# The down projection of a decoder layer by Strassen's scheme: 20 of 22 inner tiles in five chunks instead of 16 in four, on one core

## The chip, the core and the metric

The kernel runs on one core of a Trainium2 chip. The core has five engines with a queue each, which works strictly in its written order: TensorE (PE, matmuls, with its weight loads shown as PEld), VectorE (DVE), ScalarE (ACT), GpSimd (POOL) and SyncE (SP, which here only issues transfers). The metric is the device time of one execution in microseconds, the median of several runs.

## The reference

One layer of a decoder trunk for 1024 prompt tokens and 8 sample tokens (T = 1032 columns), in fp32. The part that the change is about, word for word:

```python
x = x + cross_attn(rmsnorm(x, g_attn), mk, mv, w_q, w_o)
h = rmsnorm(x, g_ffn)
x = x + (jax.nn.silu(h @ w_gate) * (h @ w_up)) @ w_down
...
y_prompt = rmsnorm(xp, g_final)
y_sample = rmsnorm(xs, g_final)
```

The model's width is 1024 (8 tiles of 128), the inner width of the feed-forward part is 2816 (22 tiles of 128). Ahead of these lines come an input projection, a causal mean pooling, a depthwise convolution of width 31 with a layer norm, the output projection, and the keys and values of 256 memory tokens.

## The kernel before, in words

**Layout.** The activations lie transposed: channels on the 128 partitions, tokens along the free dimension. Tokens come in two halves of 512 and 520. An fp32 matmul is made of three passes (`PASSES`, L133): each operand is split into a high part and a rest of type fp32r, and high x high, high x rest and rest x high are added up in PSUM. To *split* an operand costs ACT one instruction (the high part) and DVE one (the rest), both in `split` (L458, instructions at L466 and L477); `split_by_dma` (L483) lets ACT write the high part and its negative, and POOL issues a transfer that adds the original on top (L495).

**Stages in time.** Input projection, convolution, pooling, keys and values (0 to about 225 us), output projection and queries, attention (about 350 to 420), its output projection (to about 515), gate and up (to about 905), down (to about 1067), the last tiles and the final norm.

**Gate and up** work on one pair of inner tiles after the other by Strassen's seven products (`seven`, L1571; `others`, L1534). What comes out is stored by `to_hidden` (L1552): for the inner tiles below `FIRST_LAST` (L147) as the seven operand blocks `hb` that the next Strassen scheme needs, per chunk of four inner tiles; for the tiles from `FIRST_LAST` on as plain tiles `hd`. A block that is listed in `SPLIT_BLOCKS` (L58) is split there (`to_blocks`, L1504) and stored twice, high part and rest; a tile in `SPLIT_FIRST` (L59) likewise.

**Down** runs over `CHUNKS` chunks (L147) of four inner tiles, and in each over four output pairs: units u = 0 to 15, `down(u)` (L1669). A unit makes seven products `pr` (`product`, L1407, matmuls at L1429): three operands of the seven are 512 tokens wide, four are 520 wide (two matmuls of 260). A unit has 18 matmuls of 512 columns and 48 of 260. Every product is added by DVE from PSUM onto the running sums `x2` and `pp` (`plus_sums`, L1445), in the first chunk in part copied by ACT (`copy_sums`, L1449). Weights are loaded, summed (`dt`, L1631, POOL or DVE) and split (`dW`, `dV`) by `dn_load` and `dn_prep` (L1615, L1619); the blocks by `down_blocks` (L1642), which loads both parts of a block that was split ahead, and else loads it once and splits it (`hs` -> `hb`).

**The last tiles.** The inner tiles 16 to 21 go the plain way: `last_down` (L1783) multiplies them in three token spans of 512, 260 and 260 columns, for each of the 8 output tiles 18 matmuls `fd` (L1800). DVE adds the result to `x2` (L1809), ACT squares it (L512) and scales it by the final norm's gain (L1818), POOL or DVE add the squares (L513). The running sums are brought together once for each output pair by `second_half` (L1706, three DVE additions of 520 each, L1453). After each span `final_factors` (L1821) sums over channels on PE, takes the root on ACT, and three DVE instructions make the factor (L1841, L1843, L1845); `final` (L1849) multiplies on DVE (L1854) and sends `out_yT`.

**What sets the order.** A planner at the kernel's start (`Program`, L171): tasks are entered in the order of the code (`ORDER`, L41, for the first half), get a priority from their number, an offset `NUDGE` (L72) and costs with `MARGINS` (L65), some of them a fixed engine (`CHOSEN`, L119). `order` (L216) issues one after the other the task that can start first, within `SLACK` (L62) the one with the lowest priority. Buffers are taken when the task is planned; products use two PSUM buffers of three banks (`mm`) and two of one bank (`ms`). What comes out is fixed: each engine's queue is in that order.

Of the kernel before, what the change touches and what calls it, by code (L numbers as in the profile page):

```python
# [48 lines left out]
BY_DMA = {"w_in": (0, 3, 4, 6, 7, 9, 10, 11), "w_k": (2, 3, 5), "w_o": (4, 5, 6), "w_out_a": (1,), "w_out_b": (3,), "w_q": (4, 5, 6), "w_v": (0, 7), "w_dn": (18, 19), "w_dn2": (1,)}
# [1 line left out]
LEAD = {"w_k": 4, "w_v": 7, "w_out_a": 16, "w_q": 42, "w_in": 22, "w_out_b": 11, "w_o": 14}
# [1935 lines left out]
```

## Time and profile before

| | before |
|---|---|
| median of 3 runs | 1146.24 us (1144.82 to 1146.77) |
| profiled execution | 1144.27 us |
| span of the profiled execution | 1142.5 us |
| matmuls `pr` of the down stage | 288 of 512 columns, 768 of 260 |
| matmuls `fd` of the last tiles | 144 of 512 columns, 288 of 260 |

How to read it: the span goes from the first to the last record of the profiled execution; its own time is 1.8 us longer. Busy times add up an engine's records, a busy PE is not PE at its peak, and an engine's idle time only counts where others wait for it. A group's row has the line, the engine, the operation, output<-inputs, the shapes and the count, then busy us, mean ns of one, and the idle time ahead of them with what ended it.

### The profile page before, as it was taken

The numbers are of one execution on the slowest core, as the hardware profiler recorded it, in microseconds if no ns is written. First come the engines' busy times: TensorE is split into PE (matmuls) and PEld (weight loads), VectorE is DVE, ScalarE is ACT, GpSimd is POOL, SyncE is SP. The second block draws the span as 40 slices with busy tenths as digits, with TensorE's granted clock in tenths as the row PEclk, the third lists the DMA queues.
The fourth block names the chain that finished last, engine by engine and source line by source line (L and its number), as shares of the span: only waits on it lengthen the run. The fifth ranks groups of instructions, "written<-read, shape, count | busy, mean of one in ns | idle before, by whom it ended". The sixth has DMA issues, their size and how long they took to land.

```text
span 1142.5 us, 19533 instructions
## 1 busy us (share of the span) xinstructions
PE 1120.8 (98%) x7736; PEld 1067.4 (93%) x7736; DVE 927.6 (81%) x1514; ACT 499.7 (44%) x706; POOL 287.8 (25%) x327
## 2 busy tenths in 40 slices
PE   9999999999999989999999999999999999999996
PEld 8999988999999979999999999999999999999996
DVE  7999999776257886888888888988888798879744
ACT  7766648353243452445233333333433443332444
POOL 2689772133712201433000000000000123332011
PEclk9999999999999999999999999999999999999999
DMA  8444587433485687322424352254433697657612
GB/s 307 94 93 110 127 233 237 163 114 149 165 249 176 207 325 244 123 82 75 140 84 149 128 190 105 100 176 159 156 124 112 237 374 286 242 169 235 186 59 91
DMA packets 66252, 193.54 MB, mean 169 GB/s; under 512 B 8368, under 2 KB 12144, under 8 KB 64880
## 3 DMA queue, kind: packets, MB, share of 16 engines
q1 hardware_dynamic: 62128, 178.81, 43.8%
q0 software_dynamic: 3600, 13.13, 6.6%
q8 instruction: 61, 1.00, 0.4%
q10 hardware_dynamic: 432, 0.36, 0.1%
q14 instruction: 31, 0.25, 0.1%
HBM read 147.84 MB, written 44.43 MB: 168 GB/s over the span
## 4 chain that ended last, share of the span: by engine, by line
PE 78%; DVE 15%; DMA 4%; issue 1%; ACT 1%; POOL 0%; DVEq 0%; SPq 0%; ACTq 0%; POOLq 0%
PE pr L1429 49%; PE po L582 7%; DVE cacc L783 6%; PE ps L582 5%; PE fd L1800 4%; PE oa L582 4%; PE ob L582 4%; DVE spcache_k L1223 1%; PE vps L1027 1%; DMA spcache_k<-in_cache_k 1%; PE kps L949 1%; PE pv L1184 1%; DVE spcache_v L1223 1%; DVE xss L513 1%; DVE x L1854 1%
## 5 line engine op out<-in xcount | busy, mean ns | idle before, releaser
L1429 PEld LDWEIGHTS pr<-ab,wTb 128*128 128x128 f32 x1056 | 123.4, 190 | 2.3 <-issue 0.5
L1429 PE MATMUL pr<-ab,wTa 128*128 128x260 f32 x1056 | 124.9, 275 | 0.0
L1429 PE MATMUL pr<-ab,wTb 128*128 128x260 f32 x1056 | 124.3, 275 | 0.0
L1429 PEld LDWEIGHTS pr<-ab,wTa 128*128 128x128 f32 x1056 | 123.1, 190 | 1.3
L1429 PE MATMUL pr<-ab,wG 128*128 128x512 f32 x528 | 121.1, 380 | 0.0
L1429 PEld LDWEIGHTS pr<-ab,wG 128*128 128x128 f32 x528 | 96.9, 189 | 12.5 <-issue 0.5
L582 PE MATMUL ps<-xop,w 128*128 128x344 f32 x720 | 105.5, 309 | 0.0
L582 PEld LDWEIGHTS ps<-xop,w 128*128 128x128 f32 x720 | 105.0, 189 | 0.0
L1445 DVE TENSOR_TENSOR su<-pr,su 128x520 f32<-128x520 f32 (+1 forms) x112 | 77.3, 692 | 25.9 <-PE pr L1429 25.4
L1429 PEld LDWEIGHTS pr<-hb,dV 128*128 128x128 f32 x768 | 92.3, 190 | 2.2
L1429 PE MATMUL pr<-hb,dV 128*128 128x260 f32 x768 | 92.7, 275 | 0.0
L582 PE MATMUL ps<-xq,w 128*128 128x344 f32 x576 | 87.0, 310 | 0.0
L582 PE MATMUL po<-oo,w 128*128 128x344 f32 x576 | 84.7, 309 | 0.0
L582 PEld LDWEIGHTS po<-oo,w 128*128 128x128 f32 x576 | 84.3, 189 | 0.2
L582 PEld LDWEIGHTS ps<-xq,w 128*128 128x128 f32 x576 | 84.2, 189 | 0.1
L783 DVE SCALAR_TENSOR_TENSOR cacc<-glu,vec,cacc 128x502 f32<-128x502 f32 (+14 forms) x116 | 77.5, 739 | 0.1
L1429 PE MATMUL pr<-hb,dW 128*128 128x512 f32 x288 | 69.2, 379 | 0.0
L1456 POOL MEMSET su<- 128x16 f32 x22 | 2.4, 112 | 255.7 <-PE pr L1429 200.1
L1800 PE MATMUL fd<-ho,w 128*128 128x260 f32 (+1 forms) x432 | 64.3, 311 | 0.0
L1800 PEld LDWEIGHTS fd<-ho,w 128*128 128x128 f32 x432 | 59.8, 190 | 4.4 <-issue 0.5
L1445 DVE TENSOR_TENSOR x<-pr,x 128x512 f32<-128x512 f32 (+1 forms) x76 | 52.3, 690 | 12.7 <-PE pr L1429 11.6
L766 POOL TENSOR_TENSOR y<-y,cp 128x511 f32<-128x511 f32 (+14 forms) x46 | 57.6, 1254 | 14.9 <-DVE y L766 7.2
(314 smaller groups left out, 2164.7 us busy)
## 6 DMA issues: line engine op xcount, KB each, us to landing
gr<-in_w_gu SPq DMA_DIRECT2D x44, 512.0 KB, 3.4
hb<-su SPq DMA_DIRECT2D x16, 520.0 KB, 3.8
hb<-hb SPq DMA_DIRECT2D x16, 520.0 KB, 6.7
dr<-in_w_dn SPq DMA_DIRECT2D x16, 512.0 KB, 4.0
hb<-bh SPq DMA_DIRECT2D x14, 520.0 KB, 3.3
hb<-hb SPq DMA_DIRECT2D x14, 512.0 KB, 7.4
spcache_k<-in_cache_k SPq DMA_DIRECT2D x12, 512.0 KB, 5.2
ho<-hd SPq DMA_DIRECT2D x10, 520.0 KB, 6.3
```

What stands on the lines that cost most here:

```text
L513: add({"Pool": pool_tt(n), "DVE": dve(n)}, lambda e: e.tensor_tensor(total(), total(), sq[:, i, :n], ALU.add), [(sq, i), tkey], [tkey], lo ...
L582: e.matmul(placed(ps[:, c, :CW]), w[:, wi, cols], turns(x[:, xi, c * CW : (c + 1) * CW]), start=first and p == 0, stop=last and p == 2)
L766: add({"Pool": pool_tt(HALF), "DVE": dve(HALF)}, lambda e: e.tensor_tensor(yb[:, i, HALF + n : SEQ], yb[:, i, HALF + n : SEQ], cp[:, q, : ...
L783: e.scalar_tensor_tensor(acc[h][:, n:], src[:, : HALF - n], w, acc[h][:, n:], ALU.mult, ALU.add)
L949: e.matmul(placed(ps[:, 0, i * NMEM : (i + 1) * NMEM]), w[:, wi, block_cols(k)], turns(memg[k // 4][:, xi, k % 4]), start=(k == 0 and p == ...
L1027: e.matmul(placed(ps[:, m]), memg[k // 4][:, xi, k % 4, m * P : (m + 1) * P], turns(w[:, wi, col : col + 512]), start=(k == 0 and p == 0), ...
L1184: e.matmul(placed(ps[:, c]), v[:, vi, m, col : col + P], turns(pT[h][m][:, pi, sl]), start=(m == 0 and p == 0), stop=(m == 1 and p == 2))
L1223: e.scalar_tensor_tensor(piece[:, b], piece[:, b], 1.0, bc[:, b], ALU.mult, ALU.mult, accum_out=out(m)[:, first + b : first + b + 1])
L1429: e.matmul(placed(bank(c)), w[:, wi, cols(j)], turns(xs[0](j, xi)[:, c * n : (c + 1) * n]), start=onto is None and j == 0 and p == 0, stop ...
L1445: from_sums(sums, "DVE", dve, lambda e, src, sl: e.tensor_tensor(as_banks(o(sl), src), src, as_banks(a(sl), src), op), [akey], [okey])
L1800: e.matmul(placed(view(i)), w[:, wi, col : col + P], turns(hops[k][:, xi, half, lo - half * HALF + i * width // count : lo - half * HALF + ...
L1854: add({"DVE": dve(n * width)}, lambda e, i=i, n=n: e.tensor_tensor(x2[j][:, i : i + n, sl], x2[j][:, i : i + n, sl], fin[:, sl].unsqueeze( ...
```

## The change

The scheme for the down projection takes five chunks, so the tiles 0 to 19; `last_down` keeps the tiles 20 and 21, with 6 matmuls where it had 18 for each output tile and span, and the weights `w_dn2` alone. No block is split ahead (`SPLIT_BLOCKS` is empty): all 35 are loaded once as `hs` and split, 14 of them by an accumulating transfer (`DOWN_BY_DMA`). The `value` parts are no longer evicted by ACT (`EVICT`), the normalisation of the attention weights may run on ACT too, one `pv` group makes the matmuls of both token halves ahead of its copies, and the whole plan was made anew: `ORDER`, `LEAD`, `SLACK`, `MARGINS`, `NUDGE`, `CHOSEN`. Lines move down by 80 to 95. The diff, with the long tables cut:

```diff
-SPLIT_BLOCKS = ((0, 1), (0, 1, 2, 3, 6), (0, 1, 4, 5), (0, 1, 4, 5))
-SPLIT_FIRST = (16, 17, 18, 20, 21)
+EVICT = {"gate": (0,), "value": (), "mix": ()}
+DOWN_BY_DMA = (0, 2, 4, 4, 4)
+SPLIT_BLOCKS = ((), (), (), (), ())
+SPLIT_FIRST = (17, 20, 21)
+PV_MS = ()
+PV_FIRST = (4,)
-SLACK = {"Pool": 0.021, "ACT": 0.186, "DVE": 0.095, "PE": 0.044}
+SLACK = {"Pool": 0.053, "ACT": 0.174, "DVE": 0.076, "PE": 0.044}
...
-    "last": {"PE": (0.99, 0), "DVE": (1.02, 0.183)},
+    "last": {"PE": (1.02, 0.02), "DVE": (1.05, 0.243)},
...
-CHUNKS, FIRST_LAST = 4, 16
+CHUNKS = 5
+FIRST_LAST = 4 * CHUNKS
...
-    last_blocks = [("w_dn", 16), ("w_dn2", 0), ("w_dn", 17), ("w_dn", 18), ("w_dn2", 1), ("w_dn", 19)]
+    last_blocks = [("w_dn2", 0), ("w_dn2", 1)]
...
-        add({"Pool": 0.95, "DVE": 0.53}, normalise, [(st, 2), (pr, i2)], [(pr, i2)], lock=True)
+        add({"Pool": 0.95, "DVE": 0.53, "ACT": 2 * act(NMEM, ptrs=1)}, normalise, [(st, 2), (pr, i2)], [(pr, i2)], lock=True)
...
+        for step, c in ((matmuls, 0), (matmuls, 1), (copies, 0), (copies, 1)) if n in PV_FIRST else ((matmuls, 0), (copies, 0), (matmuls, 1), (copies, 1)):
+            step(c)
...
-            for f in range(FIRST_LAST, FIRST_LAST + 3):
+            for f in range(FIRST_LAST, FF_TILES):
                 later(lambda: hidden_load(f))
         down(u)
-    for f in range(FIRST_LAST + 3, FF_TILES):
-        hidden_load(f)
...
-        for w, keys, ks in ((wa, ka, range(4)), (wb, kb, (4, 5))):
-            add({"PE": pe(width // count, 3 * len(ks) * count)}, lambda e, ks=ks: emit(e, ks),
-                keys + [(hops[k], p) for k in ks for p in range(2)], [(ps,)])
+                                 start=(k == 0 and p == 0), stop=(k == 1 and p == 2))
+
+        add({"PE": pe(width // count, 6 * count)}, emit, wkeys + [(hops[k], p) for k in range(2) for p in range(2)], [(ps,)])
```

How the instructions stand on the engines shows the rest. First PE where the Strassen products end and the classical tiles begin, before the change (output<-inputs, the columns, and how many in a row; `hb` and `dW`, `dV` are operands of a Strassen product, `ho` and `w` those of a classical tile):

```order
L1429 MATMUL pr3076_10868<-hb3_2_10476,dW15_10720 128x512 x6
L1429 MATMUL pr3066_10819<-hb3_0_10427,dW15_10720 128x512 x6
L1429 MATMUL pr3074_10885<-hb3_6_10458,dV15_10656 128x260 x12
L1429 MATMUL pr3080_10906<-hb3_1_10119,dV15_10656 128x260 x12
L1800 MATMUL fd0_1_10923<-ho16_10531,w52_10816 128x512 x3
L1800 MATMUL fd0_1_10923<-ho17_10636,w52_10816 128x512 x3
L1800 MATMUL fd0_1_10923<-ho18_10734,w52_10816 128x512 x3
L1800 MATMUL fd0_1_10923<-ho19_10534,w52_10816 128x512 x3
```

And the same place of PE's queue with the change:

```order
L1893 MATMUL fd0_0_11244<-ho20_10913,w52_11099 128x512 x3
L1893 MATMUL fd0_0_11244<-ho21_11012,w52_11099 128x512 x3
L1524 MATMUL pr3160_11182<-hb4_0_10826,dW19_11127 128x512 x6
L1524 MATMUL pr3168_11261<-hb4_6_10523,dV19_11111 128x260 x12
L1524 MATMUL pr3174_11278<-hb4_1_10857,dV19_11111 128x260 x12
L1893 MATMUL fd0_1_11293<-ho20_10913,w52_11099 128x512 x3
L1893 MATMUL fd0_1_11293<-ho21_11012,w52_11099 128x512 x3
L1893 MATMUL fd0_2_11302<-ho20_10913,w52_11099 128x512 x3
L1893 MATMUL fd0_2_11302<-ho21_11012,w52_11099 128x512 x3
```

One group of the classical part (fd0_0) now stands ahead of the last three steps of products, and a group of six matmuls follows the next at once.

Second, VectorE in the first span of the last tiles, before (L1809 is the eviction of a classical tile, L1453 a Strassen combination, L513 a sum of squares):

```order
L1809 TENSOR_TENSOR x2_2_9266<-fd0_5_11047,x2_2_9266 128x512
L513 TENSOR_TENSOR fin_11013<-fin_11013,fsq0_5_11109 128x512
L1809 TENSOR_TENSOR x2_3_9345<-fd0_6_11071,x2_3_9345 128x512
L1809 TENSOR_TENSOR x2_3_9345<-fd0_7_11095,x2_3_9345 128x512
L1809 TENSOR_TENSOR x2_0_9149<-fd1_0_11126,x2_0_9149 128x260
L1809 TENSOR_TENSOR x2_0_9149<-fd1_1_11153,x2_0_9149 128x260
L1841 SCALAR_TENSOR_TENSOR fin0_t_11201<-fin0_ps0_11169,fin_11013 128x512
```

With the change (L1900 is the eviction, L1548 the combination, L594 the sum of squares):

```order
L1900 TENSOR_TENSOR x2_3_9211<-fd0_6_11346,x2_3_9211 128x512
L1900 TENSOR_TENSOR x2_3_9211<-fd0_7_11358,x2_3_9211 128x512
L1548 TENSOR_TENSOR x2_2_9170<-x2_2_9170,pp1_9178 128x520
L1548 TENSOR_TENSOR x2_2_9170<-pp1_9178 128x520
L594 TENSOR_TENSOR fin_11275<-fin_11275,fsq0_6_11387 128x512
L1548 TENSOR_TENSOR pp1_9178<-x2_3_9211,pp1_9178 128x520
L1900 TENSOR_TENSOR x2_0_9090<-fd1_0_11369,x2_0_9090 128x260
L1900 TENSOR_TENSOR x2_1_9017<-fd1_2_11379,x2_1_9017 128x260
L1548 TENSOR_TENSOR x2_3_9211<-x2_3_9211,pp1_9178 128x520
L1548 TENSOR_TENSOR x2_3_9211<-pp1_9178 128x520
```

Five of the twelve combinations of `second_half` now stand behind the eviction of fd0_7, the last of the first span; before, all twelve stood ahead of the third eviction of that span.

Third, VectorE between the second and the third span, before:

```order
L1854 TENSOR_TENSOR x2_2_9266<-x2_2_9266,fin_11013 128x2x512
L1854 TENSOR_TENSOR x2_3_9345<-x2_3_9345,fin_11013 128x2x512
L1809 TENSOR_TENSOR x2_1_9019<-fd1_3_11205,x2_1_9019 128x260
L1809 TENSOR_TENSOR x2_2_9266<-fd1_4_11230,x2_2_9266 128x260
L1809 TENSOR_TENSOR x2_2_9266<-fd1_5_11251,x2_2_9266 128x260
```

With the change:

```order
L1900 TENSOR_TENSOR x2_1_9017<-fd1_3_11458,x2_1_9017 128x260
L1900 TENSOR_TENSOR x2_2_9170<-fd1_5_11468,x2_2_9170 128x260
L1945 TENSOR_TENSOR x2_2_9170<-x2_2_9170,fin_11275 128x2x512
L1945 TENSOR_TENSOR x2_0_9090<-x2_0_9090,fin_11275 128x2x512
L1945 TENSOR_TENSOR x2_1_9017<-x2_1_9017,fin_11275 128x2x512
L1945 TENSOR_TENSOR x2_3_9211<-x2_3_9211,fin_11275 128x2x512
L594 TENSOR_TENSOR fin_11275<-fin_11275,fsq1_3_11486 128x260
L1900 TENSOR_TENSOR x2_0_9090<-fd2_0_11429,x2_0_9090 128x260
```

All evictions of the second span now stand ahead of the first span's multiplications (L1854 before, L1945 now), and those of the third span follow them.

In numbers for the whole program (before -> after): matmuls 7690 -> 7666; transfers issued by SP 373 -> 333, by POOL for the blocks 1 -> 14; blocks split after loading 13 -> 35 (DVE's part 12 -> 21); accumulations of products on DVE 44 -> 56 (x2, 512 wide), 32 -> 40 (x2, 520) and 28 -> 36 (pp, 520).

More of the change, by code (lines that the diff above doesn't have):

```diff
@@ L41 @@
 ORDER = (
[5 rows of a table removed]
[5 rows of a table added]
 )
[L49 removed]
+BY_DMA = {"w_in": (0, 1, 3, 4, 6, 7, 9, 10, 11), "w_k": (2, 3, 5), "w_o": (4, 5, 6), "w_out_a": (1,), "w_out_b": (3,), "w_q": (4, 5, 6), "w_v": (0, 7), "w_dn": (18, 19), "w_dn2": (1,)}
 WIDE = ("w_k", "w_v")
[L51 removed]
+LEAD = {"w_k": 4, "w_v": 7, "w_out_a": 11, "w_q": 30, "w_in": 13, "w_out_b": 13, "w_o": 14}
 LAST_SPANS = ((0, 512), (512, 260), (772, 260))
@@ L54 @@
 ALL_SAMPLES = (1, 6, 7)
-EVICT = {"gate": (0,), "value": (0,), "mix": ()}
-DOWN_BY_DMA = (0, 0, 0, 4)
-SPLIT_BLOCKS = ((0, 1), (0, 1, 2, 3, 6), (0, 1, 4, 5), (0, 1, 4, 5))
-SPLIT_FIRST = (16, 17, 18, 20, 21)
+EVICT = {"gate": (0,), "value": (), "mix": ()}
+DOWN_BY_DMA = (0, 2, 4, 4, 4)
+SPLIT_BLOCKS = ((), (), (), (), ())
+SPLIT_FIRST = (17, 20, 21)
 PE_FIXED, PE_COLUMN = 0.0135, 0.000417
+PV_MS = ()
+PV_FIRST = (4,)
 SCORES_MM = (5, 12, 13, 15)
-SLACK = {"Pool": 0.021, "ACT": 0.186, "DVE": 0.095, "PE": 0.044}
+SLACK = {"Pool": 0.053, "ACT": 0.174, "DVE": 0.076, "PE": 0.044}
 MARGINS = {
     "early": {"PE": (0.93, 0.0), "DVE": (0.93, 0.0), "Pool": (1.01, 0), "ACT": (1.02, 0)},
-    "gated": {"Pool": (1.04, 0.04), "DVE": (1.01, 0.02), "PE": (0.95, 0.04), "ACT": (1.08, 0.06)},
+    "gated": {"Pool": (1.01, 0.06), "DVE": (1.01, 0.04), "PE": (0.94, 0.06), "ACT": (1.09, 0.04)},
     "down": {"DVE": (1.03, 0.103)},
-    "last": {"PE": (0.99, 0), "DVE": (1.02, 0.183)},
+    "last": {"PE": (1.02, 0.02), "DVE": (1.05, 0.243)},
 }
 NUDGE = {
[45 rows of a table removed]
[115 rows of a table added]
 }
@@ L546, in w_prep @@
         name, j = seq[i]
-        w = buf(f"w{i}", "op" if name in WIDE or i >= len(seq) - 4 else "w", (P, 2, 1024), F32R)
+        w = buf(f"w{i}", "op" if name in WIDE or name == "w_dn2" else "w", (P, 2, 1024), F32R)
         if j in BY_DMA.get(name, ()):
@@ L1150, in normalise @@
             for i in range(2):
-                e.tensor_scalar(pr[:, 2 * i2 + i], pr[:, 2 * i2 + i], st[:, 6 + i : 7 + i], 1.0, ALU.mult, ALU.mult)
-        add({"Pool": 0.95, "DVE": 0.53}, normalise, [(st, 2), (pr, i2)], [(pr, i2)], lock=True)
+                at, factor = pr[:, 2 * i2 + i], st[:, 6 + i : 7 + i]
+                if e is nc.scalar:
+                    e.activation(at, at, AF.Copy, scale=factor)
+                else:
+                    e.tensor_scalar(at, at, factor, 1.0, ALU.mult, ALU.mult)
+        add({"Pool": 0.95, "DVE": 0.53, "ACT": 2 * act(NMEM, ptrs=1)}, normalise, [(st, 2), (pr, i2)], [(pr, i2)], lock=True)
     def p_transpose(n):
@@ L1174, in pv, with matmuls, emit, copies @@
         h, dt = n // 2, n % 2
-        ps = mm_buf(f"pv{n}", 2)
+        apart = [ms_buf(f"pv{n}_{c}") for c in range(2)] if n in PV_MS else []
+        ps = None if apart else mm_buf(f"pv{n}", 2)
         col, v = (h % 2) * 256 + dt * P, vv[h // 2]
         oo = oop[n]
-        for c in range(2):
+        at = lambda c: apart[c] if apart else ps
+        bank = lambda c: apart[c][:] if apart else ps[:, c]
+        def matmuls(c):
             sl = slice(c * 512, (c + 1) * 512)
-            def emit(e, c=c, sl=sl):
+            def emit(e):
                 for m in range(2):
                     for p, (vi, pi) in enumerate(PASSES):
-                        e.matmul(placed(ps[:, c]), v[:, vi, m, col : col + P], turns(pT[h][m][:, pi, sl]),
+                        e.matmul(placed(bank(c)), v[:, vi, m, col : col + P], turns(pT[h][m][:, pi, sl]),
                                  start=(m == 0 and p == 0), stop=(m == 1 and p == 2))
-            add({"PE": pe(512, 6)}, emit, [(v, 0), (v, 1)] + [(pT[h][m], p, c) for p in range(2) for m in range(2)], [(ps,)])
-            add({"ACT": act(512, True)}, lambda e, c=c, sl=sl: e.activation(halves(oo[:, 0, sl]), drawn(ps[:, c]), AF.Copy), [(ps,)], [(oo, 0, c)])
-            add({"DVE": dve(512)}, lambda e, c=c, sl=sl: e.tensor_tensor(halves(oo[:, 1, sl]), drawn(ps[:, c]), halves(f32(oo[:, 0, sl])), ALU.subtract),
-                [(ps,), (oo, 0, c)], [(oo, 1, c)])
+            add({"PE": pe(512, 6)}, emit, [(v, 0), (v, 1)] + [(pT[h][m], p, c) for p in range(2) for m in range(2)], [(at(c),)])
+        def copies(c):
+            sl = slice(c * 512, (c + 1) * 512)
+            add({"ACT": act(512, True)}, lambda e: e.activation(halves(oo[:, 0, sl]), drawn(bank(c)), AF.Copy), [(at(c),)], [(oo, 0, c)])
+            add({"DVE": dve(512)}, lambda e: e.tensor_tensor(halves(oo[:, 1, sl]), drawn(bank(c)), halves(f32(oo[:, 0, sl])), ALU.subtract),
+                [(at(c),), (oo, 0, c)], [(oo, 1, c)])
+        for step, c in ((matmuls, 0), (matmuls, 1), (copies, 0), (copies, 1)) if n in PV_FIRST else ((matmuls, 0), (copies, 0), (matmuls, 1), (copies, 1)):
+            step(c)
     def s_query(h):
@@ L1785, in last_down @@
         sl, half = slice(lo, lo + width), int(lo >= HALF)
-        (wa, ka), (wb, kb) = last_w[("w_dn", 16 + n // 2)], last_w[("w_dn2", n // 4)]
+        w, wkeys = last_w[("w_dn2", n // 4)]
         count = 1 + (width > 512)
@@ L1793, in view, with emit @@
             return ps[:, slice(count) if i is None and count > 1 else i or 0, : width // count]
-        def emit(e, ks):
-            for k in ks:
-                w, col = (wa, k * 256 + (n % 2) * P) if k < 4 else (wb, (k - 4) * 512 + (n % 4) * P)
+        def emit(e):
+            for k in range(2):
+                col = k * 512 + (n % 4) * P
                 for p, (wi, xi) in enumerate(PASSES):
@@ L1801, in emit @@
                                  turns(hops[k][:, xi, half, lo - half * HALF + i * width // count : lo - half * HALF + (i + 1) * width // count]),
-                                 start=(k == 0 and p == 0), stop=(k == 5 and p == 2))
-        for w, keys, ks in ((wa, ka, range(4)), (wb, kb, (4, 5))):
-            add({"PE": pe(width // count, 3 * len(ks) * count)}, lambda e, ks=ks: emit(e, ks),
-                keys + [(hops[k], p) for k in ks for p in range(2)], [(ps,)])
+                                 start=(k == 0 and p == 0), stop=(k == 1 and p == 2))
+        add({"PE": pe(width // count, 6 * count)}, emit, wkeys + [(hops[k], p) for k in range(2) for p in range(2)], [(ps,)])
         j, i = n // 2, n % 2
```

4 lines of the change are left out of this document (removed), and 182 rows, old and new, of tables (CHOSEN, NUDGE, ORDER).

## The prediction

> **What bounds the kernel now.** The page's first part and the busy time by stretches come first (columns: start and end, length, busy us of PE, PEld, DVE, ACT and POOL, granted clock, DMA share, GB/s).
>
> ```profile
> span 1142.5 us, 19533 instructions
> PE 1120.8 (98%) x7736; PEld 1067.4 (93%) x7736; DVE 927.6 (81%) x1514; ACT 499.7 (44%) x706; POOL 287.8 (25%) x327
> 100.00:200.00 100.00, 96.95 (x624) 90.50 (x623) 99.14 (x151) 66.67 (x86) 60.77 (x49) 0.98 0.72 197
> 350.00:420.00 70.00, 63.87 (x437) 57.99 (x437) 57.61 (x195) 35.76 (x88) 16.87 (x27) 1.00 0.63 210
> 525.00:900.00 375.00, 375.00 (x2689) 355.71 (x2688) 321.38 (x447) 134.06 (x169) 6.14 (x31) 1.00 0.38 134
> 900.00:1000.00 100.00, 100.00 (x726) 95.08 (x725) 89.32 (x128) 39.34 (x55) 29.41 (x37) 1.00 0.82 298
> 1050.00:1100.00 50.00, 50.00 (x287) 45.31 (x286) 33.35 (x50) 19.18 (x25) 3.89 (x4) 1.00 0.46 140
> 1100.00:1143.00 43.00, 33.38 (x283) 31.83 (x281) 21.98 (x42) 17.76 (x37) 7.98 (x10) 0.95 0.28 99
> ```
>
> 98% is an average over unlike stages. From 525 to 1100 PE is never idle, at a granted clock of 1.00: there a matmul saved is time saved, as long as nothing else becomes late. From 100 to 200 VectorE is the fuller engine. The last 43 us are PE's for 33 of them. The chain that ended last shows where the end comes from (start, length, engine, line, count).
>
> ```profile
> 899.85 167.58 PE pr L1429 x1205
> 1067.43 34.43 PE fd L1800 x174
> ...
> 1119.80 12.74 PE fd L1800 x114
> ...
> 1136.20 0.43 DVE x L1854
> 1136.63 0.61 DVEq L1964
> 1137.24 1.56 DVE x L1854 x3
> ```
>
> One piece is the Strassen products (L1429), the next the classical last tiles (L1800). The last Strassen product ends at 1067.43; then PE has 432 matmuls of the classical part, and VectorE finishes at 1137.24 + 1.56 = 1138.8. The span ends 3.7 later, with the last outputs' landing. The profiled execution took 1144.27, 1.8 over its span and 2.0 under the median of 1146.24. I sum against 1142.5 and add both.
>
> Does VectorE keep up in the last stage of before? Its rows (busy, mean ns, idle before them) say that it is the one that waits:
>
> ```profile
> L1809 DVE TENSOR_TENSOR x<-fd,x 128x260 f32<-128x260 f32 x16 | 6.6, 426 | 11.8 <-PE fd L1800 7.1 <-DMA out_yT<-x 4.6
> L1809 DVE TENSOR_TENSOR x<-fd,x 128x512 f32<-128x512 f32 x8 | 5.5, 692 | 11.4 <-PE fd L1800 11.4
> ```
>
> 18.5 us of waiting for PE in 24 evictions. So before is bound by PE to the end, and VectorE has a reserve there, which the change spends.
>
> **The change, part by part.** *Matmuls.* The two chain pieces give PE's pace. The first is 317 matmuls of 512 columns and 888 of 260, the second 144 and 30. Both lengths together give 0.216 us for 512 and 0.112 for 260 (the 114 of 12.74 confirm 0.112). Four inner tiles by Strassen for 1024 columns are 72 x 0.216 + 192 x 0.112 = 37.06; taken out of the last part they save 96 x 0.216 + 192 x 0.112 = 42.24. **PE: -5.2 us**, 24 matmuls of 512 columns.
>
> *The last stage.* It keeps its 24 evictions, 24 squares, 24 scalings, the sums and 13 multiplications by the final factor, but the matmuls that covered them fall from 432 to 144. VectorE's pace is in the timeline of its tail (start, length):
>
> ```profile
> 1072.26 0.69 DVE L1453 TENSOR_TENSOR x<-pp 128x520 f32<-128x520 f32 x1
> 1072.87 0.69 DVE L1453 TENSOR_TENSOR x<-x,pp 128x520 f32<-128x520 f32 x1
> ...
> 1107.44 4.62 DVE L1854 TENSOR_TENSOR x<-x,fin 128x1024 f32<-128x1024 f32 x4
> ...
> 1114.50 0.77 DVE L1809 TENSOR_TENSOR x<-fd,x 128x260 f32<-128x260 f32 x2 [2.09 <-DMA out_yT<-x]
> 1116.36 0.76 DVE L1809 TENSOR_TENSOR x<-fd,x 128x260 f32<-128x260 f32 x2 [1.09 <-DMA out_yT<-x]
> ...
> 1120.35 0.43 DVE L1841 SCALAR_TENSOR_TENSOR fin_t<-fin_ps,fin 128x260 f32<-128x260 f32 x1 [2.42 <-ACT fin L1837]
> ```
>
> Starts lie 0.61 us apart where the durations read 0.69: the pace is 0.61 for 512 or 520, about 0.345 for 260 (0.77 - 0.43), about 1.135 for 1024 ((4.62 - 1.22) / 3). By duration the sum would be 0.08 more for each instruction.
>
> Now the place from which the end is counted. The last Strassen product of the changed program ends a chunk later, plus the one classical group (6 matmuls) that PE takes ahead of it: 1067.43 + 37.06 + 1.30 = 1105.8. Seven 512-wide groups follow, 7 x 6 x 0.216 = 9.07, so the eviction of the last, fd0_7, can start at 1114.9. By the order of the changed program VectorE has 52 instructions from that eviction to its end: 17 of 512 or 520 (five of them the late Strassen combinations L1548), 31 of 260, 4 of 1024: 17 x 0.61 + 31 x 0.345 + 4 x 1.135 = 25.6. PE has left 16 x 6 x 0.112 = 10.8 and a few small sums. **VectorE sets the end**, at 1114.9 + 25.6 + 0.1 = 1140.6 if it never waits: already 1.8 behind the 1138.8 of before.
>
> It will wait a little. The rows that price it (of the page by shape, and of the outputs' landing):
>
> ```profile
> L513 POOL TENSOR_TENSOR fin<-fin,fsq 128x260 f32<-128x260 f32 x9 | 6.7, 742 | 21.5 <-ACT fsq L512 21.2
> L1832 PE MATMUL fin_ps<-fin,ones_n 128*128 128x260 f32 x4 | 1.3, 409 | 0.3 <-POOL fin L513 0.3
> L1837 ACT ACTIVATE fin<-fin_ps,eps 128x260 f32<-128x260 f32 x2 | 1.0, 479 | 0.5 <-PE fin_ps L1832 0.3 <-PE fin_ps L1835 0.3
> DMA to landing us min/median/max: 1.7/2.4/3.4
>   DVE x L1809: 4.6, 3
> ```
>
> The second span's factor needs, after VectorE's last add for it, four POOL adds, a column sum and a root: 4 x 0.74 + 0.41 + 0.48 + 0.2 of hand-overs = 4.1, beside nine 260-wide rows of VectorE (3.1): 1.0 of waiting. An eviction of the third span also waits until the first span's output of the same tile has landed (4.6 us in before, three times). Four other instructions now stand between, the second tile goes first, and the wait for the factor covers part: I take 0.8 between 0 and 4.6. Hand-overs in the other chains: 0.4. Together 2.2: last VectorE instruction at 1142.8, span 1146.5. **The last stage costs +4.0, PE's saving included.**
>
> [...]
>
> *The down stage until then.* The fifth chunk gives VectorE 28 more accumulations (28 x 0.61 = 17.1) and four tiles' weight splits. Since no block is split ahead any more, VectorE splits 21 blocks after loading where it split 12, and POOL issues 14 accumulating transfers where it issued 1.
>
> ```profile
> L477 DVE TENSOR_TENSOR hb<-hs,hb 128x1040 fp32r<-128x1040 f32 x7 | 9.2, 1309 | 0.4 <-ACT hb L466 0.4
> L495 POOL DMA_DIRECT2D hb<-hb x1 | 0.9, 873 | 0.0
> L477 DVE TENSOR_TENSOR dV<-dt,dV 128x1024 fp32r<-128x1024 f32 x16 | 19.5, 1219 | 0.6 <-ACT dV L466 0.5
> L466 ACT ACTIVATE dV<-dt 128x1024 fp32r<-128x1024 f32 x16 | 16.9, 1057 | 37.5 <-POOL dt L1631 28.3 <-PE pr L1429 4.6 <-DVE dt L1631 3.8
> ```
>
> Nine more splits are 9 x 1.2 = 11 us spread over five chunks; ACT's 22 more are 23 us, on an engine busy for 39 of 100. A chunk asks of VectorE 28 x 0.61 + 4 x (1.135 + 0.61 + 0.37) + 4 splits x 1.2 = 30.3 of 37 us, against 89.32 of 100 by durations in the last rows of before: PE stays covered, and I take **0**. The splits ahead disappear from gate and up (16 instructions of 1024 or 1040 on each of VectorE and ACT), where PE had no wait: also 0. 40 fewer transfers are issued by SP, and the DMA share was 0.82 where it was highest: 0. If this cover is gone, PE loses what VectorE is late: up to the 11 us.
>
> *Before 525.* PE stood still, by name, in these places, and VectorE's largest early group is the convolution:
>
> ```profile
> PE pv L1184 <- DVE oo L1189: 2.5, 4, 1.5
> PE vps L1027 <- DVE kf L953: 1.9, 1, 1.9
> PE sc L1126 <- ACT probs L1143: 1.6, 1, 1.6
> PE psv L582 <- ACT w L466: 1.1, 1, 1.1
> L783 DVE SCALAR_TENSOR_TENSOR cacc<-glu,vec,cacc 128x502 f32<-128x502 f32 (+14 forms) x116 | 77.5, 739 | 0.1
> ```
>
> With the smaller ones some 12 us. The convolution keeps its 116 instructions, K's and V's matmuls only change places (kps2 now goes ahead of a vps1), and the scores come in the same order. pv 4 does both halves before its copies, and ten of the 32 normalising instructions go to ACT: a part of the 2.5 and of the 1.6. On the other side an added wait holds whatever is next in an engine's queue. Bounds: -6 (half of the 12) and +3; I take 0.
>
> **The sum:** -5.2 on PE, but VectorE's end moves 1138.8 -> 1142.8; span 1142.5 + 4.0 = 1146.5, its own execution 1148.3, the median **1150.2**.
>
> **The rivals.** (1) *VectorE keeps up, PE's saving shows*: it would have to run its 52 instructions inside PE's 10.8 us and the final chain; if combinations and evictions were done by then, the median is 1146.24 - 5.2 = 1141. For it: 18.5 us of reserve in before. Against: the sum of 25.6, and rows that overlap already. (2) *The new plan wins back waits before 525*: 4 of the 12 us cancel the tail, and the time stays near 1146; 6 or more would show as a gain, 1144. For: pv 4 and the moved normalisations sit on named waits. Against: VectorE is 99.14 busy of 100 between 100 and 200, and its instructions there are nearly the same. (3) *The other side, beyond my forecast: the late splits.* VectorE's nine more splits of 1.2 us stand in one queue with the accumulations that free PSUM. Whatever of the last chunk's accumulations, combinations and splits is not done when its last product ends adds whole to the 25.6, for nothing after it has idle time to give: four splits' worth gives +5 on top, 1155. It decides as soon as VectorE is over 2.4 us behind there (seven groups of PE in 9.07 us stand against eleven VectorE instructions of 0.61, 6.7). For: 30.3 of 37 us are asked in every chunk, and the last one's combinations come late. Against: VectorE catches up in 6.7 us of every chunk. (4) *The change does not do what it says* is excluded for the counts (24 fewer of 512 columns in the changed program); what it can miss is their place on the path, and that is the forecast.
>
> **How the numbers follow.** A measurement tells about 0.2% (2.3 us) from no change, so faster is under 1143.9 and slower above 1148.5. Forecast 0.52 (its own range 1147.5 to 1153), rival 1 0.08, rival 2 0.23 (a quarter of it under 1143.9), rival 3 0.17. Slower: 0.17 and five sixths of 0.52, 0.60. Faster: 0.08 and 0.06, 0.14. The same: the rest, 0.26. The range from 1143.5 to 1155 leaves out rival 1 and the ends of 2 and 3.
>
> **What would show it.** Right: the last Strassen product ends near 1106; VectorE's rows from the eviction of fd0_7 to the end are back to back, with idle time below 5 us and hardly any of it for PE; PE's fd rows wait for VectorE (L1900), for the first time; the last 40 us have PE well under 80% busy. Wrong: a last product much before 1104 or after 1108 (then the early part or the down stage moved), VectorE idle for PE in the last 30 us (rival 1), or PE idle for L1540 or for splits between 900 and 1100 (rival 3).

## The result, and the profile after

The changed kernel takes **1162.23 us** (median of 4 runs, 1161.66 to 1168.68) where the kernel before takes 1145.64 (4 runs, the three of above among them): a ratio of **1.0156 [1.0139, 1.0173]**, 1.6% slower. Forecast were 1150.2, in a range from 1143.5 to 1155. The direction was right, the size wrong by 12 us. The profiled execution took 1162.2 us, 1.8 over its span, as before.

The page of the changed kernel, its first lines:

```profile
span 1160.4 us, 19501 instructions
PE 1122.8 (97%) x7712; PEld 1068.2 (92%) x7712; DVE 955.3 (82%) x1559; ACT 507.2 (44%) x723; POOL 306.3 (26%) x349
```

24 matmuls fewer, as counted; yet PE's busy time has risen by 2.0, and VectorE's by 27.7. The busy time by stretches (columns as for the kernel before):

```profile
100.00:200.00 100.00, 94.02 (x602) 87.73 (x601) 99.29 (x147) 66.40 (x84) 58.00 (x48) 0.98 0.69 188
...
900.00:1000.00 100.00, 98.97 (x705) 93.20 (x704) 93.48 (x129) 58.23 (x75) 30.77 (x37) 1.00 0.85 261
1050.00:1100.00 50.00, 49.16 (x348) 45.97 (x347) 45.37 (x67) 19.31 (x25) 13.01 (x18) 1.00 0.55 156
1100.00:1161.00 61.00, 41.52 (x248) 37.00 (x246) 48.25 (x84) 24.70 (x48) 13.08 (x14) 0.85 0.24 78
1135.00:1140.00 5.00, 0.30 (x1) 0.30 (x2) 4.31 (x6) 1.42 (x5) 1.30 (x2) 0.88 0.86 322
1140.00:1145.00 5.00, 5.00 (x24) 5.00 (x24) 2.39 (x6) 2.66 (x7) 2.73 (x6) 0.50 0.26 98
```

Between 100 and 200 PE is 2.9 us less busy than before. In two stretches of the down stage it now has gaps (98.97 of 100, 49.16 of 50), where it had none. And in the last stage it does almost nothing for 5 us, then runs 5 us at a granted clock of **0.50**. The waits of PE by name (total, times, longest):

```profile
PE fd L1893 <- DVE x L1900: 7.3, 3, 5.4
PE kps L1030 <- DVE a L1016: 4.0, 1, 4.0
PE fin_ps L1923 <- DVE fin L594: 2.4, 1, 2.4
...
PE pr L1524 <- DVE hb L558: 1.0, 1, 1.0
...
PE pr L1524 <- DVE pp L1540: 0.8, 1, 0.8
```

The 7.3 in the last tiles and the 1.0 and 0.8 in the down stage were not there before. That in the keys (`kps`) was, at 0.9 (waits of PE, kernel before):

```profile
PE kps L949 <- DVE a L935: 0.9, 1, 0.9
```

The chain that ended last, from 1090 on, has the start of the last stage, and the timeline of PE has the first product of gate and up (start, length):

```profile
1110.47 3.98 PE pr L1524 x30
1114.44 9.08 PE fd L1893 x42
...
1154.46 1.83 DVE x L1945 x3
```

```profile
516.23 4.05 PE L1524 MATMUL pr<-ab,wG 128*128 128x512 f32 x18
```

The same line of before reads

```profile
510.63 7.29 PE L1429 MATMUL pr<-ab,wG 128*128 128x512 f32 x33
```

That splits the span into three parts.

| part | before | forecast | after | over the forecast |
|---|---|---|---|---|
| to the first product of gate and up | 510.63 | 510.63 | 516.23 | 5.6 |
| from there to the end of the last Strassen product | 556.80 | 595.16 | 598.21 | 3.05 |
| from there to the end of the span | 75.07 | 40.7 | 45.96 | 5.3 |

(556.80 is 1067.43 - 510.63; the forecast adds the fifth chunk's 37.06 and 1.30; after, 1114.44 - 516.23.) The excess is 13.9 of span. By the medians it is 12.0: the forecast added 2.0 from a profiled run to the median, and the changed kernel's profiled run lies at its median.

### The profile page after: what moved, and what is told of

The parts are those of the page before. It is cut to its first block, busy times and chain, and to the rows that moved or that the text cites. A ratio compares the mean times of both kernels' runs of the same rounds, so it can differ in the third digit from the quotient of the medians.

```text
span 1160.4 us, 19501 instructions
## 1 busy us (share of the span) xinstructions
PE 1122.8 (97%) x7712; PEld 1068.2 (92%) x7712; DVE 955.3 (82%) x1559; ACT 507.2 (44%) x723; POOL 306.3 (26%) x349
## 4 chain that ended last, share of the span: by engine, by line
PE 75%; DVE 15%; DMA 5%; issue 4%; ACT 1%; POOL 0%; ACTq 0%; DVEq 0%; SPq 0%; POOLq 0%
PE pr L1524 50%; PE po L663 7%; DVE cacc L864 6%; PE ps L663 5%; PE ob L663 4%; PE oa L663 3%; DMA spcache_k<-in_cache_k 2%; PE fd L1893 2%; DVE spcache_k L1318 1%; PE psv L663 1%; PE psg L663 1%; DMA w<-in_w_out_a 1%; DVE spcache_v L1318 1%; PE pv L1273 1%; DMA sbcache_v<-pd 1%
## 5 line engine op out<-in xcount | busy, mean ns | idle before, releaser
L1524 PEld LDWEIGHTS pr<-hb,dV 128*128 128x128 f32 x960 | 115.7, 190 | 5.8 <-DVE pp L1540 1.2
L1524 PE MATMUL pr<-hb,dV 128*128 128x260 f32 x960 | 116.8, 275 | 1.9 <-DVE hb L558 1.0
L1524 PE MATMUL pr<-hb,dW 128*128 128x512 f32 x360 | 87.1, 380 | 0.0
L1540 DVE TENSOR_TENSOR x<-pr,x 128x512 f32<-128x512 f32 (+1 forms) x96 | 65.5, 690 | 9.7 <-PE pr L1524 8.7
L1524 PEld LDWEIGHTS pr<-hb,dW 128*128 128x128 f32 x360 | 63.8, 189 | 7.0 <-issue 0.2
L1524 PE MATMUL pr<-ab,wU 128*128 128x512 f32 x264 | 60.6, 379 | 0.0
```

The costliest lines, as they stand in the source:

```text
L1524: e.matmul(placed(bank(c)), w[:, wi, cols(j)], turns(xs[0](j, xi)[:, c * n : (c + 1) * n]), start=onto is None and j == 0 and p == 0, stop ...
L1540: from_sums(sums, "DVE", dve, lambda e, src, sl: e.tensor_tensor(as_banks(o(sl), src), src, as_banks(a(sl), src), op), [akey], [okey])
```

## The experiments

All kernels were timed beside the kernel before in the same session (its median 1144.5 to 1146.45). e1 and e2 exchange the tables of the plan. All others start from the changed kernel, take the order that its planner returns, and move single tasks in it or give a task to another engine; the queues keep their order otherwise. In these, lines lie 14 further down than in the changed kernel, in e1 140 and in e2 141 further up. Executions of one kernel lie up to 7 us apart here, so an effect of 2 or 3 us is read from its stage in the profile, beside the median. Such a stage comes from one profiled execution for each kernel.

**Is it the plan or the scheme?** e1_old_early_plan has five chunks, but the plan of before for all tasks up to the attention's output projection; e2_new_early_plan_four is its counterpart, four chunks with the change's early plan.

```diff
-    "n0 g1 C0 v1 g2 v2 s0 m1 g3 A1 A3 m7 s1 m6 v3 m3 m0 m5 m4 D0 A0 A2 m2 K0 W3 C1 s3 K1 s2 K2 V1 W0 W1 D1 M3 C2 W2 M0 Y0 V0 "
+    "n0 g1 C0 v1 g2 s0 m6 v2 m1 g3 s1 m3 A1 A3 v3 m7 m4 m5 D0 A0 A2 m0 m2 K0 W3 C1 s3 K1 s2 K2 V1 W0 W1 C2 W2 M0 D1 Y0 M3 V0 "
...
-PV_FIRST = (4,)
+PV_FIRST = ()
...
-                pick, slack = None, SLACK.get(e, 0.02)
+                pick, slack = None, SLACKS[len(issued) >= 1670].get(e, 0.02)
```

(This is e1's, against the changed kernel; e2's is the reverse, against the kernel before.)

> Five chunks with the early half planned as before (the tables for the tasks up to the output projection of the attention are those of before, the tables behind them those of the change; the queues from the down stage to the end are the changed kernel's, row for row). Theory 'three places' (the new plan loses 5.6 us before 516, the down stage 3, the last stage the rest): 1162.2 - 5.6 = 1156.6, the first gate matmul near 510.6, and the last stage as long as in the changed kernel (46.0 us from the last Strassen product to the span's end). Rival 'all of it is the five chunks' (the early loss is only shifted work that the later stages wait for anyway): 1161 to 1163.

> The complement: four chunks and the classical six tiles as before, with the changed kernel's early plan (its tables for the tasks up to the output projection of the attention, those of before behind). Theory 'three places': 1145.6 + 5.6 = 1151.2, the first gate matmul near 516.2. Rival 'all of it is the five chunks': 1145 to 1147.

Measured: e1 1158.75 us, ratio 1.0108 [1.0091, 1.0125]; e2 1152.28, ratio 1.0047 [1.0030, 1.0065]. 1.08% and 0.47% make 1.55%, the 1.56% of the whole change: **the fifth chunk costs 1.1%, the new early plan 0.5%**, and they add up. e2 lies 1.1 above its figure; it shows the same 4.0 of waiting as the changed kernel, behind the same long instruction (waits of PE, then VectorE's timeline):

```profile
PE kps L889 <- DVE a L875: 4.0, 1, 4.0
```

```profile
136.39 4.30 DVE L742 TENSOR_TENSOR ysum<-y 128x1032 f32<-128x1032 f32 x1
```

e1 missed its figure by 2.1. Its first product of gate and up starts at 512.56, 3.7 before that of the changed kernel, but its last Strassen product ends only 1.0 earlier: from gate to the last product it takes 600.9, where the other runs with five chunks take 597.5 to 600.2. Its last stage takes 44.2 and not 46.0, with the same queues there; the clock, below, explains a part of that (the 24 matmuls take 5.01 and not 5.57). And 512.56 is not the 510.63 of before, though the plan is the same. What differs most is a wait for a load of the K cache, 0.5 in before:

```profile
PE ss L1191 <- DVE spcache_k L1178: 3.4, 1, 3.4
```

This wait changes from execution to execution: with the change's early plan and equal queues it was 1.8 in the changed kernel, 3.7 in e3 and 0.3 in e7. It can be one of the reasons for the spread of the medians.

**The early wait.** VectorE's `ysum` (L883), a 1032-wide addition, took 4.30 us. Beside it stood, on POOL, the first step of a pooling window (L993 to L995), which before was VectorE's; the later steps (L990, L991) were POOL's before, too. VectorE's timeline of the changed kernel, and POOL's:

```profile
137.52 4.30 DVE L883 TENSOR_TENSOR ysum<-y 128x1032 f32<-128x1032 f32 x1
...
146.40 1.23 DVE L1016 TENSOR_TENSOR a<-ps,Rx 128x1032 f32<-128x1032 f32 x1
```

```profile
137.92 1.57 POOL L994 TENSOR_TENSOR win<-a 128x511 f32<-128x511 f32 x1
139.15 1.58 POOL L995 TENSOR_TENSOR win<-a 128x512 f32<-128x512 f32 x1
140.79 1.09 POOL L990 COPY win<-win 128x2 f32<-128x2 f32 x1
...
143.79 0.19 POOL L990 COPY win<-win 128x4 f32<-128x4 f32 x1
```

POOL's two additions end at 140.73, and VectorE's ends 1.09 later, at 141.82. In these 1.09 POOL has a copy of two columns that takes 1.09, where the next such copy takes 0.19. Read so, VectorE's addition stood still until POOL's two were through, and then held up POOL. Behind it in VectorE's queue waits the eviction L1016, for which PE stands still. e5_window_on_dve gives that window step back to VectorE (407 is the task), and e6_eviction_first leaves it on POOL and moves seven VectorE instructions of the convolution from ahead of the eviction to behind it, just ahead of task 760.

```diff
+    MOVES = []
+    for n, t, e in rearranged(pg, MOVES, {407: 'DVE'}):
```

```diff
+    MOVES = [(754, 'before', 760), (714, 'before', 760), (755, 'before', 760), (756, 'before', 760), (757, 'before', 760), (758, 'before', 760), (759, 'before', 760)]
```

> The changed kernel; only the first step of the pooling window of group 3 (two additions of 511 and 512) runs on VectorE, where POOL did them. In the changed kernel VectorE's sum ysum took 4.30 us at 137.5 beside these additions, where the form's median is 1.23, and PE then waited 4.0 us for the eviction (L1016) behind it. Theory 'a run of POOL instructions holds VectorE's': ysum takes 1.2 to 2.2 us, the two additions cost VectorE 1.3, the eviction starts 1 to 2 us earlier, PE's wait falls to 2 to 3 us, the whole 1 to 2 us faster (1160.5 to 1161). Rival 'ysum is slow for a reason of its own': it stays at 4.3, PE's wait grows to 5.3, 1163.5.

> The changed kernel; only seven VectorE instructions of the convolution, queued ahead of the eviction L1016 for which PE waits 4.0 us at 143.5, stand behind it. Theory 'the wait is a matter of queue order': PE's wait falls below 0.5 and the whole is 3 to 4 us faster (1158.5). Rival 'VectorE is the fuller engine there': the wait goes, but comes back in the waits for K's and the windows' evictions up to 190 us, since VectorE has as much to do; output projection at most 1 us earlier, 1161.5 to 1162.5.

Measured: e5 1158.26, ratio 1.0107 [1.0086, 1.0128], 4.0 us below the changed kernel, more than was expected; e6 1163.67, ratio 1.0159 [1.0139, 1.0179], nothing gained, and above both of its figures. In e5 VectorE's timeline reads

```profile
136.86 1.23 DVE L897 TENSOR_TENSOR ysum<-y 128x1032 f32<-128x1032 f32 x1
...
143.92 1.22 DVE L1030 TENSOR_TENSOR a<-ps,Rx 128x1032 f32<-128x1032 f32 x1
```

VectorE has two 0.7 instructions and one of 0.15 more here, and is 2.5 earlier at the eviction. The first product of gate and up starts at 513.26, 3.0 earlier. Over all profiles: with the step on POOL it starts between 513.57 and 517.10 (the changed kernel, e3, e4, e7, e8: mean 515.95), with the step on VectorE between 511.17 and 513.26 (e5, e9, e10: mean 512.5). **The step on POOL costs 3.5** by these means. The wait for the K cache differs between the two groups as well (mean 2.0 and 1.1); without it the starts are 512.7 to 515.1 and 511.0 to 511.7, and the step costs 2.6. In e6 the wait only changes its name:

```profile
PE kps L1044 <- DVE kf L1048: 6.8, 1, 6.8
```

So VectorE was what was full there (99.29 of 100 in its row), and the order of its work gains nothing; the time in which POOL kept it from running does. Of the 5.6 in this execution, then, 2.6 are the step and 1.3 the wait for the K cache (1.8 here, 0.5 before). The remaining 1.7 were not traced to one edit; the eviction starts at 142.41 in the kernel before and at 143.92 in e5, so a part of its delay belongs to the rest of the plan.

**The last stage.** Two parts of its excess were tried. VectorE's four 1024-wide multiplications (L1945) stand ahead of the third span's evictions, and PE waits 5.4 for these. e3_products_later puts the four, with their outputs, behind those evictions. e4_keep_clock leaves the order and gives PE 24 matmuls of 512 columns after fd1_5, into a spare PSUM bank that nobody reads.

```diff
+    MOVES = [(3241, 'after', 3322), (3242, 'after', 3241), (3237, 'after', 3302), (3238, 'after', 3237), (3239, 'after', 3312), (3240, 'after', 3239), (3243, 'after', 3332), (3244, 'after', 3243)]
```

```diff
+        if n == 3269:
+            spare = next(b for b in pg.tasks[3306].bufs if b.name == "fd2_2").tile
+            for _ in range(24):
+                nc.tensor.matmul(placed(spare[:, 2]), last_w[("w_dn2", 0)][0][:, 0, :P], turns(hops[0][:, 0, 0, :512]), start=True, stop=True)
```

> The changed kernel; only the four first-span products (L1945, 1024 wide) and their output transfers stand later in VectorE's queue: each behind the third span's two evictions of its own tile. Theory 'a queue order starves PE, and PE comes back at half clock': PE's wait of 5.4 us for L1900 falls below 1.5, the granted clock stays near 1.00 until 1145, the waits for landing outputs (1.3) go: 3 to 5 us faster, 1157.5 to 1159. Rival 'the sum of VectorE's work is the limit': VectorE has the same instructions, so at most the 1.3 of landing waits, 1161.

> The changed kernel with 24 more matmuls of 512 columns on PE ahead of the matmul that waits 5.4 us for an eviction in the last stage (their result, in a spare PSUM bank, is read by nobody). No other queue changes. Theory 'half clock': PE is busy through the gap, the granted clock stays 1.00 from 1135 to 1145 where it was 0.50 from 1140 on, the 24 matmuls of the third span behind it take 2.7 us where they took 5.57: 2 to 3 us faster, 1159.5 to 1160. Rival 'PE's pace there does not matter': 1162, or later by what the added matmuls hold up.

Measured: e3 1159.21, ratio 1.0113 [1.0098, 1.0128], just above its theory's range; e4 1157.46, ratio 1.0102 [1.0084, 1.0120], a larger gain than its theory's. From the last product to the end of the span e3 takes 42.6 and e4 42.9, where the changed kernel takes 45.96. First the changed kernel's timeline of PE there, then e4's (windows, then timeline):

```profile
1133.39 0.94 PE L1893 MATMUL fd<-ho,w 128*128 128x260 f32 x6 [0.39 <-DVE x L1900]
1139.70 5.57 PE L1893 MATMUL fd<-ho,w 128*128 128x260 f32 x24 [5.38 <-DVE x L1900]
...
1149.17 1.24 PE L1923 MATMUL fin_ps<-fin,ones_n 128*128 128x260 f32 x2 [2.45 <-DVE fin L594]
```

```profile
1135.00:1140.00 5.00, 5.00 (x27) 4.44 (x26) 4.90 (x6) 1.46 (x5) 0.04 (x2) 1.00 0.58 216
1140.00:1145.00 5.00, 4.01 (x31) 3.41 (x31) 3.41 (x9) 4.38 (x12) 4.76 (x7) 1.00 0.55 207
```

```profile
1134.18 5.34 PE L1995 MATMUL fd<-ho,w 128*128 128x512 f32 x24
1141.07 3.02 PE L1907 MATMUL fd<-ho,w 128*128 128x260 f32 x24 [0.87 <-DVE x L1914]
```

With PE kept busy, the clock stays at 1.00, and the same 24 matmuls take 3.02 where they took 5.57. So **the clock explains 3.1 of the 5.3** in this execution: VectorE, late already, waits for a PE at half speed. It is no fixed price. In the last stage e1, e5, e6 and e7 have the changed kernel's queues on every engine, and take 44.2, 46.0, 44.1 and 46.0 there. In the changed kernel PE starts again 0.9 after the clock has fallen, and the 24 matmuls take 5.57, as they do in e5 and e7; in e1 it starts 2.5 after the fall (granted clock 0.62 from 1135 to 1140), and they take less (timeline of PE in e1; in e6 4.82):

```profile
1138.73 5.01 PE L1753 MATMUL fd<-ho,w 128*128 128x260 f32 x24 [5.39 <-DVE x L1760]
```

Against e4's 42.9 and e9's 43.2 these last stages are between 0.9 and 3.1 longer, read here as the price of the half clock. e3 gains 3.3 in another way: PE waits 3.5 in five pieces, none over 1.5, and its clock falls only at about 1141.8, when most is done.

e8_tail_relieved went further: the order of e3, eight sums of squares moved from VectorE to POOL, three scalings from POOL to ACT, and ten matmuls that nobody reads at the end.

```diff
+    for n, t, e in rearranged(pg, MOVES, {3196: 'Pool', 3201: 'Pool', 3209: 'Pool', 3222: 'Pool', 3252: 'Pool', 3262: 'Pool', 3304: 'Pool', 3309: 'Pool', 3248: 'ACT', 3300: 'ACT', 3315: 'ACT'}):
```

> The changed kernel with its last stage relieved: the first span's products behind the third span's evictions (as in the run with products later), eight of VectorE's sums of squares on POOL, three scalings on ScalarE in place of POOL, and ten matmuls nobody reads behind the last classical group on PE, to keep its clock. Theory 'VectorE's queue sets the end, at 0.35 to 0.61 us an instruction': 3 to 4 us less work on VectorE, on top of the 3 us of the products' order: 1154 to 1156. Rival 'the sums' chain on POOL (0.74 and 1.3 each) becomes the end': 1158 to 1160.

Measured: 1162.78, ratio 1.0152 [1.0137, 1.0168], 3.6 above e3 and above both of its figures. PE now waits for the chain of sums on POOL, and VectorE's combinations, 0.69 alone, stretch beside it (waits of PE; timelines of VectorE and POOL):

```profile
PE fin_ps L1937 <- POOL fin L608: 2.9, 1, 2.9
```

```profile
1125.07 1.79 DVE L1562 TENSOR_TENSOR x<-pp 128x520 f32<-128x520 f32 x1
1124.81 3.17 POOL L608 TENSOR_TENSOR fin<-fin,fsq 128x512 f32<-128x512 f32 x2 [0.33 <-ACT fsq L607]
```

Work taken from VectorE cost VectorE time here, as POOL did it at the same moment. How much of the 3.6 is this, how much the longer chain on POOL and how much a stretch of half clock (last section) was not separated.

**The down stage.** VectorE's split of a block at 1070 took 3.49 us beside three additions of POOL, and PE waited 0.8 for the eviction behind it (rows of VectorE and of POOL in the changed kernel's timeline; in e7, where they start behind POOL's run, two such splits took 2.37):

```profile
1070.13 1.06 POOL L1726 TENSOR_TENSOR dt<-dt,dr 128x256 f32<-128x256 f32 x1
1070.15 3.49 DVE L558 TENSOR_TENSOR hb<-hs,hb 128x1024 fp32r<-128x1024 f32 x1
1070.83 1.04 POOL L1726 TENSOR_TENSOR dt<-dr 128x256 f32<-128x256 f32 x1
1071.52 1.03 POOL L1726 TENSOR_TENSOR dt<-dr,dt 128x256 f32<-128x256 f32 x1
```

e7_splits_behind moves this split behind the eviction that it held up, and the split at 933, for which PE waited 1.0, two places ahead on ACT and VectorE.

```diff
+    MOVES = [(3055, 'before', 3058), (2550, 'before', 2566), (2551, 'before', 2569)]
```

> The changed kernel; only three moves in the down stage: the split of the first chunk's last 520-wide block (hb0_6) two places ahead on ScalarE and VectorE, and the split of the last chunk's hb4_2 behind the eviction that it holds at 1070. Theory 'late splits hold PE': the waits of 1.1 us at 933 and 1.0 at 1073 and the idle time around them go, the last Strassen product 2 to 3 us earlier, 1159.5 to 1160. Rival 'VectorE has no room there': the waits move to the next products, 1162.

Measured: 1161.84, ratio 1.0157 [1.0128, 1.0187], no gain. Both waits are gone by name, and others stand in their place:

```profile
PE pr L1538 <- DVE x L1554: 2.1, 3, 1.3
...
PE pr L1538 <- DVE dW L572: 1.4, 1, 1.4
```

From the first product of gate and up to the end of the last it is 600.2, against 598.2. Moved by order alone, the waits only change their place.

**Do the cures add up?** e9_clock_and_window joins e4 and e5; e10_order_and_window joins e3 and e5, with 6 and 14 matmuls that nobody reads behind fd2_5 and fd2_7, in the gaps of its third span.

```diff
-        if n == 3269:
-            spare = next(b for b in pg.tasks[3306].bufs if b.name == "fd2_2").tile
-            for _ in range(24):
+        if n == 3321:
+            spare = next(b for b in pg.tasks[3316].bufs if b.name == "fd2_4").tile
+            for _ in range(6):
...
+        if n == 3331:
+            spare = next(b for b in pg.tasks[3326].bufs if b.name == "fd2_6").tile
+            for _ in range(14):
```

(e10 against e9; the order of e3 is in it besides.)

> The changed kernel with two edits that each helped alone: the 24 matmuls nobody reads in PE's gap (4.8 us alone) and the first window step on VectorE (4.0 us alone). Theory 'three places' (the losses lie in different stages and add up): 1162.2 - 4.8 - 4.0 = 1153.4, that is 1152 to 1155; the last Strassen product near 1111, and 43 us from there to the span's end. Rival 'the gains are the spread of the executions': 1157 or more.

> The changed kernel with the products later (3.0 us alone), the first window step on VectorE (4.0), and 6 and 14 matmuls nobody reads on PE behind its last groups. Theory 'half clock also prices the sums at the end': the last two column sums on PE run at the full clock (0.7 us in place of 1.24 and 1.07), 1 us more than the sum of the two: 1153.5 to 1155.5. Rival 'VectorE's queue is the limit there': no more than the two, 1155 to 1156.5.

Measured: e9 1156.22, ratio 1.0096 [1.0065, 1.0127]; e10 **1155.12**, ratio 1.0085 [1.0061, 1.0109]. e9's median lies between the two theories' figures; by stages the gains add up: its last product ends at 1109.48, 5.0 earlier than in the changed kernel (1.6 of this is the wait for the K cache, 0.2 here and 1.8 there), and the rest takes 43.2, 2.7 less. e10's median fits both of its theories, and the profile has to tell them apart. In e10 the rest takes 41.7, 1.0 over the forecast, with the last column sums of `fin` at full speed (timeline of PE; they took 1.24 in the changed kernel):

```profile
1142.11 0.71 PE L1937 MATMUL fin_ps<-fin,ones_n 128*128 128x260 f32 x2 [0.90 <-DVE fin L608]
```

e10 is the best of these versions. It is still 0.85% slower than the kernel before, and none of them beats it.

## Why the prediction was right and wrong, point by point

The forecast lay 12 us too low. Three steps of its sum failed, and all three put a wait at nothing or near it: "before 525" at 0 (it cost 5.6), the down stage at 0 (it cost 3.05), and in the last stage VectorE's waiting for PE, "hardly any of it" (2.6, in a stage 5.3 over its forecast).

**PE -5.2: right as a count, and worth nothing on the path.** 24 matmuls are gone, the seven groups of the first span took 9.08 (forecast 9.07), and PE is busy for 21.1 of the last 40 us. The last product ended at 1114.44, not at 1105.8; 1108 had been named as the sign that an earlier part had moved, and it had.

**VectorE sets the end: right, but not alone.** From the start of fd0_7's eviction, 1123.5, to its last instruction's end, 1156.3, VectorE takes 32.8 where the sum gave 25.6 of work and 2.2 of waiting. PE's fd rows wait for L1900 for the first time, as forecast. Here are the two groups of that time ahead of which VectorE stood idle (groups by shape; behind the last bar, the idle time and who ended it):

```profile
L1900 DVE TENSOR_TENSOR x<-fd,x 128x260 f32<-128x260 f32 x16 | 6.5, 425 | 4.0 <-PE fd L1893 2.6 <-DMA out_yT<-x 1.3
...
L1932 DVE SCALAR_TENSOR_TENSOR fin_t<-fin_ps,fin 128x260 f32<-128x260 f32 x2 | 0.9, 429 | 1.7 <-ACT fin L1928 1.7
```

Idle are 5.7, not "below 5": 1.3 for landings where 0.8 was taken, 1.7 for ACT's root where 1.0 was, and 2.6 for PE, for which a share of 0.4 was. The step that failed is that last one: *"hardly any of it for PE"*. The sum gave PE its full pace whenever VectorE needed it, but the four multiplications (4.62, the same as before) made PE wait 5.4, PE lost its clock, and then VectorE waited for a slow PE. Of the 5.0 that the 32.8 lie over 27.8, 3.5 are such waits, and the rest is work: where VectorE stands still between two instructions, each takes its full duration and not the pace of a queue (0.43 and not 0.345 for 260 columns), and one combination took 1.09 for 0.69. **The last stage was forecast at +4.0 and cost +9.25**; keeping the clock gives back 3.1 of the difference (e4), and would give back less in an execution like e1's.

**The down stage at 0: wrong by 3.05.** The cover was argued from a mean, 30.3 of 37 us in a chunk. By mean it holds (93.48 of 100, 45.37 of 50), but a queue that is 90% full had no room at the moment that counted: one block's split, 3.49 long instead of 1.2, held up an eviction. That is rival 3's mechanism, but in the middle of the stage and not behind it, and 3 of the 11 us that were its price without any cover. 1.8 of it stand in the two waits above; e7 shows that another order alone brings nothing, and whether fewer splits on VectorE would was not tried.

**Before 525 at 0: wrong by 5.6, the largest term.** It had bounds of -6 and +3, and the loss lies outside them. The estimate counted instructions ("nearly the same") and the waits that the plan might remove; it did not ask what stands *beside* them. The window step given to POOL saves VectorE two instructions of 0.7, but held its addition for 3.1, in a stretch where VectorE is 99% busy; giving it back restores 2.6 to 3.5 (e5, e9, e10). The wait for the K cache, 1.3 of the 5.6, is the spread of executions and no step of the forecast. Rival 2's gains were real where they were sought (the `pv` wait fell from 2.5 to 1.2) and were lost in this.

**The rivals and the range.** Rivals 1 (the saving shows) and 2 (a gain early) are out. The range was built from cases taken one by one. A longer tail, late splits and an early loss came all three at once, and the early loss, for which its part had a bound of +3, was no rival of its own.

## What to carry to other kernels

Before work is taken from the engine that bounds a stage, ask what the next engine does there at each moment, not on average: here VectorE was 91 to 99% busy, and single delays of it reached the path. An instruction's cost here was not its own: beside POOL's additions one of VectorE's took 4.30 us for 1.23, another 3.49 for 1.22. So price a move from VectorE to POOL at the place where it lands. And where a fast engine is made to wait in a kernel's last stage, price its slow restart too: the 24 matmuls behind PE's gap of 5.38 us took 5.57, and 3.02 where the gap was filled.
